# Weight-tile sums by accumulating loads from DRAM, with the seven products in another order

## The chip, the cores and the metric

The kernel runs on one core of a Trainium2 chip. The metric is the device time of one execution, in microseconds (us). Each kernel is run several times and the median is given. One further execution is taken with the hardware profiler; its page and its trace are what the sections below read. The engines are called PE (TensorE, the matrix unit), DVE (VectorE), ACT (ScalarE), POOL (GpSimd) and SP (SyncE) in the profile. SyncE, ScalarE and GpSimd can issue DMA transfers, each on a queue of its own; the transfers of all queues run on the same 16 DMA engines.

## The reference

One layer of a decoder trunk with 256 positions and a width of 2048. All numbers are float32. Cut to what matters here:

```python
h = rmsnorm(x, norm_g)
proj = einsum('bsd,df->bsf', h, w_in)              # 2048 -> 18432, split among four branches
...
ya, yb, yc, yd = ...                               # four token mixers, each times its SiLU gate
yproj = einsum('bsnc,ncd->bsnd', branches, w_branch)
gates = sigmoid(einsum('bsd,df->bsf', h, w_gate) + b_gate)    # 2048 -> 4 * 2048
merged = sum(gates * yproj, axis=2)
out = rmsnorm(x + einsum('bsd,de->bse', merged, w_out), final_g)
```

The change touches the products of `h` with `w_gate` (8192 columns) and with the columns of `w_in` that make the values `a_v` and `c_v` (1024 each).

## The kernel before

**Tiles and precision.** The weights lie in DRAM as tiles of 128 x 2048 float32, 1 MB each. `load_weights` brings one into a buffer of the pool `st`, which has six, on SyncE's queue. TensorE multiplies in float32r, so each operand is cut into a high and a low half by `split` (lines 96 to 98): ScalarE copies the tile to `hi` with rounding, and VectorE takes `lo = st - hi`. There are three buffers for each half. A product is then made of three: high by high, high by low and low by high.

**The products with seven multiplications.** `group` (line 324) computes a block of 256 rows by 1024 columns of `h` times a weight matrix of 2048 rows. It sees both operands as 2 x 2 blocks and uses a scheme of the Strassen-Winograd kind with seven products in place of eight. Four combinations of the blocks of `h` (`s1`, `s2`, `s3`, `n4`) are made once, by `make_sx`. The combinations of the weight blocks are made anew in each group: `tile_of(c, h, j)` loads half `j` of the weight block in row half `h` and column half `c`, and `add_to` (line 340) adds another loaded tile to one that is already in `st`, by one VectorE instruction over 128 x 2048. There are eight such sums in a group, and 12 loads: blocks (1,0) and (1,1), as (c,h), are loaded twice. The sum `ts[j]` is kept for the whole group, and changed in place three times: it starts as block (0,0), and then (1,0), (1,1) and (0,1) are added in turn. A second sum, `t3`, is block (1,0) plus block (1,1).

Every product is two calls of `half` (line 331), each with 12 matmuls of 128 x 512. The products gather in the PSUM banks `X`, `Y` and `Z`; `keep` copies a bank away by ScalarE, and `done` makes the final sums of an output block and hands them to `sink`, which applies the function and writes the result to DRAM (`g_dr` on ScalarE's queue for the gates, `v_dr` on GpSimd's queue for the values).

**The order of work.** `group` is a generator: each `yield` ends a step. Ten groups (eight for the gates, one each for `a_v` and `c_v`) stand in `queue`. The main program goes through the branches; `proj_t` makes the transposed projections, each tile with 32 matmuls, and `branch` multiplies a branch with `w_branch`. Between their tiles they call `step(n)`, which runs the next n steps of the group at the head of the queue. So TensorE's order is written out by hand, in the order in which the program is traced. The order on the other engines comes from a scheduler that follows priorities: `tc.high_priority(SPLIT_AHEAD)` moves splits ahead by 100, `ADD_AHEAD` the sums by 140.

**The other queues.** GpSimd's queue carries the branch values (`y_dr`, `cn`, `yf`, `v`), the gates fetched back (`gl`) and the running sum of the branches (`m_dr`, `ml`). ScalarE's queue carries the gates to DRAM. A queue issues in order: what waits holds up what stands behind it.

Of the kernel before, what the change touches and what calls it, by code (L numbers as in the profile page):

```python
# [9 lines left out]
F32 = mybir.dt.float32  # L10
F32R = mybir.dt.float32r
AF = mybir.ActivationFunctionType
ALU = mybir.AluOpType
AX = mybir.AxisListType

P = 128
# [20 lines left out]
def weight_plan():  # L37

    plan = []
    for n in ("b_a", "b_b", "b_g", "a_q", "a_k", "a_g", "c_u", "c_g", "d_g", "d_q", "d_k"):  # L40
        plan += [("in", OFF[n] // P + i) for i in range(24 if n in ("d_q", "d_k") else 8)]
    for n in ("d_v", "a_v", "c_v"):
        plan += [("inN", OFF[n] // 512 + c, q) for c in range(2) for q in range(4)]
    plan += [("gateN", g, q) for g in range(16) for q in range(4)]
    plan += [("brN", b, c, q) for b in range(4) for c in range(4) for q in range(2)]
    plan += [("out", c, q) for c in range(4) for q in range(4)]
    return plan
# [10 lines left out]
def hybrid_block(ctx: ExitStack, tc, w, x, xT, vec, bg, cst, dmask, sgu_wT, sgu_lg, sgu_lb, sgu_b, final_g, out):  # L58
    nc = tc.nc
    V, A, T = nc.vector, nc.scalar, nc.tensor  # L60
# [16 lines left out]
    ps_n = ctx.enter_context(tc.tile_pool(name="psn", bufs=2, space=bass.MemoryType.PSUM))  # L77
# [4 lines left out]
    index = {e: n for n, e in enumerate(weight_plan())}  # L82
    used = set()

    def load_weights(expect, pieces=1, between=None, again=False):
        assert again == (expect in used), expect
        used.add(expect)
        st = st_p.tile([P, 2048], F32, tag="st", name="st")
        n = 2048 // pieces
        for c in range(pieces):  # L90
            nc.sync.dma_start(st[:, c * n:(c + 1) * n], w[index[expect]][:, c * n:(c + 1) * n])
            if between is not None:
                between(c)
        return st
# [11 lines left out]
    def split_tile(st):  # L106
        hi, lo = new_hi(), new_lo()
        with tc.high_priority(SPLIT_AHEAD):
            split(hi, lo, st[:])
        return hi, lo  # L110
# [207 lines left out]
    def x_part(name):  # L318
        if name in ("a11", "a12", "a22"):
            k0, t0 = (0 if name == "a11" else KB), (P if name == "a22" else 0)  # L320
            return lambda k, part: xhl[:, k0 + k, part * S + t0:part * S + t0 + P]
        return lambda k, part: sx[name][:, part, k, :]

    def group(expect, sink, bias=None):


        def tile_of(c, h, j):
            e = expect(c, 2 * h + j)
            return load_weights(e, again=e in used)

        def half(ps, st, name, j, first, last):
            lh = x_part(name)
            hi, lo = split_tile(st)
            for kk in range(4):
                k, o = 4 * j + kk, kk * 512
                for i, (part, w_) in enumerate(((0, hi), (0, lo), (1, hi))):
                    T.matmul(ps[:], lh(k, part), w_[:, o:o + 512], start=first and j == kk == i == 0,  # L337
                             stop=last and j == 1 and kk == 3 and i == 2, skip_group_check=name not in ("a11", "s1", "a12"))

        def add_to(st, other):  # L340
            with tc.high_priority(ADD_AHEAD):
                V.tensor_add(st[:], st[:], other[:])  # L342

        def keep(ps, name):
            t = so_p.tile([P, 512], F32, tag="so", name=name)
            with tc.high_priority(SPLIT_AHEAD):
                A.activation(t[:], ps[:], AF.Copy)
            return t

        def done(tb, c, op, a, b, t):  # L350
            with tc.high_priority(SPLIT_AHEAD):
                if op is not None:
                    op(t[:], a[:], b[:])
                sink(tb, c, t, op is not None)

        X = ps_x.tile([P, 512], F32, tag="x", name="X")
        if bias is not None:
            T.matmul(X[:], sel[:, bias:bias + 1].to_broadcast([P, P]), bgr[:], start=True, stop=False)
        ts = []
        for j in range(2):  # L360
            ts.append(tile_of(0, 0, j))
            half(X, ts[j], "a11", j, bias is None, True)
            yield
        p1 = keep(X, "p1")
        Z = ps_n.tile([P, 512], F32, tag="n", name="Z")
        if bias is not None:
            T.matmul(Z[:], sel[:, bias + 8:bias + 9].to_broadcast([P, P]), bgr[:], start=True, stop=False)
        for j in range(2):
            add_to(ts[j], tile_of(1, 0, j))
            half(Z, ts[j], "s1", j, bias is None, True)  # L370
            yield
        p5 = keep(Z, "p5")
        for j in range(2):
            add_to(ts[j], tile_of(1, 1, j))
            half(X, ts[j], "s2", j, False, True)
            yield
        u2 = keep(X, "u2")
        for j in range(2):
            t3, b22 = tile_of(1, 0, j), tile_of(1, 1, j)
            half(Z, b22, "n4", j, False, True)  # L380
            add_to(t3, b22)
            yield
            half(X, t3, "s3", j, False, True)
            if j == 0:
                yield
        done(0, 1, V.tensor_sub, Z, u2, u2)
        done(1, 1, V.tensor_sub, p5, X, p5)
        yield
        Y = ps_n.tile([P, 512], F32, tag="n", name="Y")
        for j in range(2):  # L390
            b21 = tile_of(0, 1, j)
            half(Y, b21, "a12", j, True, True)
            add_to(ts[j], b21)
            yield
            half(X, ts[j], "a22", j, False, True)
            if j == 0:
                yield
        done(0, 0, V.tensor_add, Y, p1, p1)
        done(1, 0, None, X, X, X)
        yield  # L400

# [31 lines left out]
    def gate_group(b, cc):  # L433
        bi = BRANCH[b]

        def sink(tb, c, t, in_sbuf):
            g = t if in_sbuf else so_p.tile([P, 512], F32, tag="so", name="g")
            A.activation(g[:], t[:], AF.Sigmoid)
            o = (2 * cc + c) * 512
            nc.scalar.dma_start(g_dr[bi, tb, :, o:o + 512], g[:])  # L440

        return group(lambda c, q: ("gateN", bi * 4 + 2 * cc + c, q), sink, bias=bi * 2 + cc)

    def v_group(name, func):
        def sink(tb, c, t, in_sbuf):
            g = t if in_sbuf else so_p.tile([P, 512], F32, tag="so", name="g")
            if func is not None or not in_sbuf:
                A.activation(g[:], t[:], func or AF.Copy)
            nc.gpsimd.dma_start(v_dr[name][:, tb, c * 512:(c + 1) * 512], g[:])

        return group(lambda c, q: ("inN", OFF[name] // 512 + c, q), sink)
# [395 lines left out]
    for q in range(4):  # L847
        st = load_weights(("out", 3, q))
# [75 lines left out]
```

## Time and profile before

| | us |
|---|---|
| median of 3 runs | 1586.61 |
| lowest and highest run | 1583.34, 1593.16 |
| the profiled execution | 1585.26 |
| its span (first to last instruction) | 1583.4 |

The profiled execution's mean TensorE clock was 0.969 of full speed. In the profile's groups a line reads: line of the kernel, engine, operation, output and inputs, shape, count, then busy time and mean duration, then the idle time of the engine just ahead of them and what ended it. In a list of waits, a row says which instruction waited for which, for how many us in total, how often, and the longest. In a list of DMA issues, the last column is the median time from issue to landing. In the rows of DMA queues stand the packets, the MB moved (10^6 bytes) and the time that the packets took as a share of 16 engines over the span. Matmuls are pipelined: the duration of one is longer than the distance to the next.

### The profile page before, as it was taken

The numbers are of one execution on the slowest core, as the hardware profiler recorded it, in microseconds if no ns is written. First come the engines' busy times: TensorE is split into PE (matmuls) and PEld (weight loads), VectorE is DVE, ScalarE is ACT, GpSimd is POOL, SyncE is SP. The second block draws the span as 40 slices with busy tenths as digits, with TensorE's granted clock in tenths as the row PEclk, the third lists the DMA queues.
The fourth block names the chain that finished last, engine by engine and source line by source line (L and its number), as shares of the span: only waits on it lengthen the run. The fifth ranks groups of instructions, "written<-read, shape, count | busy, mean of one in ns | idle before, by whom it ended". The sixth has DMA issues, their size and how long they took to land.

```text
span 1583.4 us, 18121 instructions
## 1 busy us (share of the span) xinstructions
PE 1465.1 (93%) x7204; PEld 1225.5 (77%) x7204; DVE 1241.8 (78%) x1232; ACT 864.5 (55%) x777; POOL 87.5 (6%) x159
## 2 busy tenths in 40 slices
PE   7999999999999999869999999989989899959897
PEld 6788887888887777658788788867768688847786
DVE  7799999555799998867788788898889777866454
ACT  6544444353457567644466766766554477744251
POOL 0100000000000000010100000000211200011000
PEclk9999999999999999989999999989999999979999
DMA  9655543555166768677876757677898877578441
GB/s 358 217 211 186 186 176 136 180 180 181 59 237 257 283 249 289 212 276 275 283 282 224 241 213 279 239 260 256 301 337 297 328 274 248 196 282 299 167 161 54
DMA packets 62836, 370.89 MB, mean 234 GB/s; under 512 B 8128, under 2 KB 8256, under 8 KB 24096
## 3 DMA queue, kind: packets, MB, share of 16 engines
q1 hardware_dynamic: 44640, 313.68, 54.9%
q0 software_dynamic: 12784, 46.61, 8.8%
q10 hardware_dynamic: 5328, 9.45, 1.7%
q8 instruction: 56, 0.92, 0.2%
q14 instruction: 28, 0.23, 0.0%
HBM read 343.50 MB, written 26.21 MB: 233 GB/s over the span
## 4 chain that ended last, share of the span: by engine, by line
PE 62%; DVE 14%; DMA 10%; issue 7%; ACT 6%; POOL 0%; DVEq 0%; ACTq 0%; POOLq 0%; SPq 0%
PE ps L219 24%; PE ps L222 12%; DVE lo L98 8%; PE X L337 7%; DMA st<-in_w_dram 6%; ACT hi L97 3%; DVE st L342 3%; PE Z L337 3%; PE Y L337 2%; PE pso L261 2%; PE pso L260 2%; PE pso L259 2%; PE psy L259 1%; PE psy L260 1%; PE psy L261 1%
## 5 line engine op out<-in xcount | busy, mean ns | idle before, releaser
L98 DVE TENSOR_TENSOR lo<-st,hi 128x2048 fp32r<-128x2048 f32 (+2 forms) x318 | 711.6, 2247 | 165.7 <-ACT hi L97 164.9
L97 ACT ACTIVATE hi<-st 128x2048 fp32r<-128x2048 f32 (+2 forms) x318 | 595.0, 1879 | 231.4 <-PE psy L261 83.1
L219 PE MATMUL ps<-xhl,hi 128*128 128x512 f32 x1920 | 691.8, 403 | 6.3 <-ACT vd L523 3.8
L222 PE MATMUL ps<-xhl,lo 128*128 128x256 f32 x1920 | 523.4, 283 | 11.3 <-DVE lo L98 11.3
L219 PEld LDWEIGHTS ps<-xhl,hi 128*128 128x128 f32 x1920 | 361.6, 190 | 86.8 <-ACT vd L523 4.2
L222 PEld LDWEIGHTS ps<-xhl,lo 128*128 128x128 f32 x1920 | 366.2, 191 | 24.3 <-DVE lo L98 14.8
L242 ACT ACTIVATE bt<-ps 128x256 f32<-128x256 f32 x120 | 46.0, 384 | 331.0 <-PE ps L219 329.4
L342 DVE TENSOR_TENSOR st<-st 128x2048 f32<-128x2048 f32 x80 | 182.9, 2287 | 33.9 <-DMA st<-in_w_dram 33.5
L337 PE MATMUL X<-hi,xhl 128*128 128x512 f32 x320 | 109.2, 406 | 12.8 <-ACT hi L97 10.9
L337 PE MATMUL X<-hi,s 128*128 128x512 f32 x320 | 106.0, 393 | 0.9 <-ACT hi L97 0.9
L259 PE MATMUL psy<-hi,yh 128*128 128x512 f32 x256 | 100.6, 393 | 5.2 <-DVE ml L792 4.7
L260 PE MATMUL psy<-lo,yh 128*128 128x512 f32 x256 | 100.7, 393 | 1.6 <-DVE lo L98 1.6
L261 PE MATMUL psy<-hi,yl 128*128 128x512 f32 x256 | 100.2, 392 | 0.0
L243 DVE TENSOR_TENSOR dst<-ps,bt 128x256 f32<-128x256 f32 x120 | 50.5, 420 | 61.9 <-ACT bt L242 61.5
L543 DVE SCALAR_TENSOR_TENSOR cv<-glu,vec_sb,cv 128x246 f32<-128x246 f32 (+27 forms) x240 | 98.8, 462 | 0.2
L337 PEld LDWEIGHTS X<-hi,xhl 128*128 128x128 f32 x320 | 63.2, 197 | 27.2 <-ACT hi L97 11.6
L337 PE MATMUL X<-lo,xhl 128*128 128x512 f32 x160 | 65.1, 407 | 7.0 <-DVE lo L98 7.0
L337 PEld LDWEIGHTS X<-hi,s 128*128 128x128 f32 x320 | 60.7, 190 | 13.5 <-ACT hi L97 1.3
L337 PE MATMUL X<-lo,s 128*128 128x512 f32 x160 | 63.5, 397 | 5.6 <-DVE lo L98 5.6
L337 PE MATMUL Y<-hi,xhl 128*128 128x512 f32 x160 | 59.0, 432 | 3.4 <-ACT hi L97 3.4
L337 PE MATMUL Z<-hi,s 128*128 128x512 f32 x160 | 53.7, 400 | 8.7 <-ACT hi L97 8.7
L259 PEld LDWEIGHTS psy<-hi,yh 128*128 128x128 f32 x256 | 48.4, 189 | 16.3 <-DVE ml L792 4.9
(248 smaller groups left out, 1531.6 us busy)
## 6 DMA issues: line engine op xcount, KB each, us to landing
st<-in_w_dram SPq DMA_DIRECT2D x294, 1024.0 KB, 5.4
gl<-g_dr POOLq DMA_DIRECT2D x32, 256.0 KB, 6.8
m_dr<-gl POOLq DMA_DIRECT2D x24, 256.0 KB, 6.1
ml<-m_dr POOLq DMA_DIRECT2D x24, 256.0 KB, 6.3
g_dr<-p ACTq DMA_DIRECT2D x16, 256.0 KB, 4.5
g_dr<-u ACTq DMA_DIRECT2D x8, 256.0 KB, 5.2
g_dr<-g ACTq DMA_DIRECT2D x8, 256.0 KB, 3.9
xr<-in_x_dram POOLq DMA_DIRECT2D x8, 256.0 KB, 4.4
```

The lines of the kernel that those rows point to most:

```text
L97: A.activation(hi, src, AF.Copy)
L98: V.tensor_sub(lo, src, hi.bitcast(F32))
L219: T.matmul(ps[:], hi[:, o:o + P], rhs[:, k, :], start=start, stop=stop)
L222: T.matmul(ps[:, 0:S], lo[:, o:o + P], rhs[:, k, 0:S], start=False, stop=False)
L242: A.activation(bt[:], ps[:, S:2 * S], AF.Copy)
L243: V.tensor_add(dst[:, j, :], ps[:, 0:S], bt[:])
L259: T.matmul(ps[tb][:], lh(k0 + kk, 0, tb), hi[:, o:o + 512], start=st, stop=False)
L260: T.matmul(ps[tb][:], lh(k0 + kk, 0, tb), lo[:, o:o + 512], start=False, stop=False)
L261: T.matmul(ps[tb][:], lh(k0 + kk, 1, tb), hi[:, o:o + 512], start=False, stop=sp)
L337: T.matmul(ps[:], lh(k, part), w_[:, o:o + 512], start=first and j == kk == i == 0, stop=last and j == 1 and kk == 3 and i == 2, skip_grou ...
L342: V.tensor_add(st[:], st[:], other[:])
L543: V.scalar_tensor_tensor(dst, src, wc, dst, op0=ALU.mult, op1=ALU.add)
```

## The change

`add_to` no longer loads a tile and adds it on VectorE. It issues one DMA on GpSimd's queue that reads the tile from DRAM and adds it to what lies in the buffer. The tile that is added is no longer loaded by itself, so a group has 8 plain loads and 8 accumulating ones. Such a transfer may start only when the split of the old content has been read, and the next split waits for it to land.

The products are put in another order. The accumulation for the next use of `ts[j]` is issued right after the step that used it. The product `a12`, which needs no sum, moves from the end to the second place, and its output block is finished there. `n4` and the second sum are cut into two halves, `p3(0)` and `p3(1)`, ahead of and behind `s2`; both tiles of the second sum are kept in `t3s` until `s3`. Block (1,1) is now fetched three times: plainly for `n4`, and by an accumulating load for each of the two sums; before it was fetched twice.

```diff
-        def add_to(st, other):
+        def add_to(st, c, h, j):
+            e = expect(c, 2 * h + j)
+            used.add(e)
             with tc.high_priority(ADD_AHEAD):
-                V.tensor_add(st[:], st[:], other[:])
+                nc.gpsimd.dma_start(st[:], w[index[e]], accum_op=ALU.add)
...
-        ts = []
+        ts, t3s = [], []
         for j in range(2):
             ts.append(tile_of(0, 0, j))
             half(X, ts[j], "a11", j, bias is None, True)
+            add_to(ts[j], 1, 0, j)
             yield
         p1 = keep(X, "p1")
+        Y = ps_n.tile([P, 512], F32, tag="n", name="Y")
+        for j in range(2):
+            half(Y, tile_of(0, 1, j), "a12", j, True, True)
+            if j == 0:
+                yield
+        done(0, 0, V.tensor_add, Y, p1, p1)
+        yield
         Z = ps_n.tile([P, 512], F32, tag="n", name="Z")
...
         for j in range(2):
-            add_to(ts[j], tile_of(1, 0, j))
             half(Z, ts[j], "s1", j, bias is None, True)
+            add_to(ts[j], 1, 1, j)
             yield
         p5 = keep(Z, "p5")
+        def p3(j):
+            half(Z, tile_of(1, 1, j), "n4", j, False, True)
+            t3s.append(tile_of(1, 0, j))
+            add_to(t3s[j], 1, 1, j)
+
+        p3(0)
+        yield
         for j in range(2):
-            add_to(ts[j], tile_of(1, 1, j))
             half(X, ts[j], "s2", j, False, True)
+            add_to(ts[j], 0, 1, j)
             yield
         u2 = keep(X, "u2")
+        p3(1)
+        yield
+        done(0, 1, V.tensor_sub, Z, u2, u2)
         for j in range(2):
-            t3, b22 = tile_of(1, 0, j), tile_of(1, 1, j)
-            half(Z, b22, "n4", j, False, True)
-            add_to(t3, b22)
-            yield
-            half(X, t3, "s3", j, False, True)
+            half(X, t3s[j], "s3", j, False, True)
             if j == 0:
                 yield
-        done(0, 1, V.tensor_sub, Z, u2, u2)
         done(1, 1, V.tensor_sub, p5, X, p5)
         yield
-        Y = ps_n.tile([P, 512], F32, tag="n", name="Y")
         for j in range(2):
-            b21 = tile_of(0, 1, j)
-            half(Y, b21, "a12", j, True, True)
-            add_to(ts[j], b21)
-            yield
             half(X, ts[j], "a22", j, False, True)
             if j == 0:
                 yield
-        done(0, 0, V.tensor_add, Y, p1, p1)
         done(1, 0, None, X, X, X)
         yield
```

## The prediction

> **What bounds the kernel now.** The times of each engine on the page come first, to see which one could be the limit.
>
> ```profile
> PE 1465.1 (93%) x7204; PEld 1225.5 (77%) x7204; DVE 1241.8 (78%) x1232; ACT 864.5 (55%) x777; POOL 87.5 (6%) x159
> ```
>
> TensorE is busy for 93% of the span. Next I asked for the costs by line on VectorE, with a window. The sums that the change removes are the group of line 342; all 80 lie between 468 and 1410 us, so everything below is about these 942 us.
>
> ```profile
> L98 DVE TENSOR_TENSOR lo<-st,hi 128x2048 fp32r<-128x2048 f32 x215 | 489.0, 2287 | 81.8 <-ACT hi L97 81.4
> L342 DVE TENSOR_TENSOR st<-st 128x2048 f32<-128x2048 f32 x80 | 182.9, 2287 | 33.9 <-DMA st<-in_w_dram 33.5
> ```
>
> The third view is the waits of TensorE alone in that window, which tells what VectorE's load costs the engine that is nearly full.
>
> ```profile
> PE Y L337 <- DVE lo L98: 13.7, 5, 3.8
> PE ps L222 <- DVE lo L98: 11.3, 8, 2.8
> PE X L337 <- DVE lo L98: 10.7, 8, 2.2
> PE Z L337 <- ACT hi L97: 8.7, 1, 8.7
> PE Z L337 <- DVE lo L98: 7.2, 7, 1.9
> ```
>
> TensorE waits for a low half from VectorE (line 98) for 13.7 + 11.3 + 10.7 + 7.2 = 42.9 us in all. That is the most that a lighter VectorE can give back directly, although it loses 182.9 us of work. The last view is the busy time in six equal stretches, with the share of the DMA engines, and then the same stretches for line 342 alone.
>
> ```profile
> 468.00:625.00 157.00, 146.13 (x707) 120.48 (x706) 144.36 (x119) 107.91 (x96) 3.85 (x7) 0.99 0.76 272
> 625.00:782.00 157.00, 134.15 (x590) 108.57 (x588) 119.84 (x67) 77.10 (x56) 14.81 (x27) 0.95 0.72 260
> 782.00:939.00 157.00, 153.35 (x776) 130.15 (x777) 128.06 (x82) 103.50 (x90) 2.38 (x4) 0.98 0.72 253
> 939.00:1096.00 157.00, 145.01 (x699) 120.27 (x698) 131.40 (x86) 111.81 (x91) 5.27 (x9) 0.96 0.68 241
> 1096.00:1253.00 157.00, 149.14 (x644) 121.09 (x643) 134.39 (x98) 75.56 (x49) 31.65 (x56) 0.98 0.90 318
> 1253.00:1410.00 157.00, 145.09 (x733) 122.29 (x731) 119.18 (x92) 103.47 (x95) 12.18 (x21) 0.96 0.70 251
> ...
> 468.00:625.00 157.00, 39.91 (x18) 0.99 0.76 272
> 625.00:782.00 157.00, 33.15 (x15) 0.95 0.72 260
> 782.00:939.00 157.00, 29.74 (x13) 0.98 0.72 253
> 939.00:1096.00 157.00, 31.32 (x14) 0.96 0.68 241
> 1096.00:1253.00 157.00, 25.89 (x12) 0.98 0.90 318
> 1253.00:1410.00 157.00, 22.87 (x10) 0.96 0.70 251
> ```
>
> The columns are TensorE, its weight loads, VectorE, ScalarE and GpSimd busy, the clock, the DMA share and GB/s; the last six rows have VectorE's column alone, with the number of sums in brackets (18, 15, 13, 14, 12, 10, together 82: two stand across an edge and count twice). The reader should see that no engine is idle here: the DMA engines already work 0.68 to 0.90 of the time. The change takes work from VectorE and gives it to them.
>
> **The change, part by part.** *The removed sums.* 80 instructions at 2.287 us leave VectorE, 182.9 us. It was not the last to finish except in the 42.9 us above, so this is worth 0 to 42.9 us, and only where nothing else becomes the limit.
>
> In VectorE's program, at the first group of sums (`lo` is a low half, `st` a loaded weight tile, `cv` the convolution), it stands before:
>
> ```order
> L342 TENSOR_TENSOR st<-st 128x2048
> L98 TENSOR_TENSOR lo<-st,hi 128x2048
> L159 TENSOR_SCALAR rs<-rs 128x256
> L243 TENSOR_TENSOR dst<-ps,bt 128x256
> L342 TENSOR_TENSOR st<-st 128x2048
> L98 TENSOR_TENSOR lo<-st,hi 128x2048
> ```
>
> and now:
>
> ```order
> L98 TENSOR_TENSOR lo<-st,hi 128x2048
> L159 TENSOR_SCALAR rs<-rs 128x256
> L160 TENSOR_TENSOR rs<-rs 128x256
> L243 TENSOR_TENSOR dst<-ps,bt 128x256
> L646 TENSOR_TENSOR cv<-cv,rs 128x2048
> L98 TENSOR_TENSOR lo<-st,hi 128x2048 x4
> ```
>
> The splits now follow each other with nothing of the sums between them.
>
> *The loads.* Each of the ten groups loaded 12 tiles of 1 MB on SyncE's queue, and now loads 8, so 40 plain loads go; in their place come 80 accumulating loads on GpSimd's queue. The queue rows price a plain one.
>
> ```profile
> q1 hardware_dynamic: 44640, 313.68, 54.9%
> q0 software_dynamic: 12784, 46.61, 8.8%
> q10 hardware_dynamic: 5328, 9.45, 1.7%
> ```
>
> SyncE's queue (q1) took 0.549 x 1583.4 = 869 us of all 16 engines for 313.68 MB: 2.77 us per MB, or 2.90 us for a tile of 1.049 MB. Where the engines are full, they are a little quicker:
>
> ```profile
> 12.00:42.00 30.00, 26.94 (x117) 21.18 (x116) 25.94 (x28) 19.88 (x25) 0.00 (x0) 1.00 0.99 393
> ...
> 1126.00:1220.00 94.00, 87.73 (x370) 70.97 (x369) 79.00 (x50) 46.99 (x31) 18.75 (x35) 0.96 0.93 329
> ```
>
> At 393 GB/s a tile takes 2.67 us. No accumulating load is in this trace. It must read the tile from DRAM, read the old values from SBUF, and write the sum. From below, the second read costs nothing beside the first: 2.67 us. From above, the two reads and the write each take a pass of their own: 8.0 us. The nearest row for a read of SBUF is ScalarE's queue (q10), whose transfers go from SBUF to DRAM: 0.017 x 1583.4 / 9.45 = 2.85 us per MB, as dear as a read from DRAM. I therefore take two reads in series at the full-engine rate, 2 x 2.67 = 5.3 us, and keep both ends.
>
> [...]
>
> *The sum.* In a stretch with n sums the DMA work becomes share x 157 - (n/2) x 2.90 + n x 5.3 = share x 157 + 3.85 n: 188.6, 170.8, 163.1, 160.7, 187.5 and 148.4 us. Beyond 157 it cannot fit, and the engines do not stay full: the longest full stretch above, 1126 to 1220 us, has 0.93, the short one 0.99. I divide by 0.95: 198.5, 179.8, 171.7, 169.1, 197.4 and 156.2. Over 157 that is 41.5 + 22.8 + 14.7 + 12.1 + 40.4 + 0 = 131.5 us. Where the DMA engines are the limit, the 42.9 us of VectorE are no gain. The span becomes 1583.4 + 131.5 = 1715; the profiled execution took 1585.26 us, 1.9 beyond its span, and lies 1.3 under the median 1586.61. Against the median, 1718 us.
>
> *GpSimd's queue.* Its program at the same place, where `y_dr` and `cn` are branch values stored and fetched, was:
>
> ```order
> L462 DMA y_dr_d<-dst 128x512
> L462 DMA y_dr_b<-cv 128x2048
> L658 DMA cn<-y_dr_b 128x512
> L462 DMA y_dr_b<-dst 128x512
> L658 DMA cn<-y_dr_b 128x512
> ```
>
> and is now:
>
> ```order
> L344 DMA st<-in_w_dram 128x2048
> L471 DMA y_dr_d<-dst 128x512
> L344 DMA st<-in_w_dram 128x2048
> L471 DMA y_dr_b<-cv 128x2048
> L344 DMA st<-in_w_dram 128x2048 x11
> L667 DMA cn<-y_dr_b 128x512
> L344 DMA st<-in_w_dram 128x2048 x3
> ```
>
> The accumulating loads (line 344) stand in one row with the stores and fetches of the branches, and each waits until its tile was split. An issue costs GpSimd what it does now:
>
> ```profile
> L484 POOL DMA_DIRECT2D gl<-g_dr x32 | 17.2, 541 | 60.1 <-DMA m_dr<-gl 35.1 <-PE pt L788 16.1 <-DMA v_dr_c_v<-p 4.2
> ```
>
> 80 x 0.541 = 43 us on an engine that is 6% busy: 0 on the path. SyncE loses 40 issues of an engine that does nothing else, worth 0. What stands behind a waiting accumulation (`gl`, `ml`, `cn`) is late by at most that wait.
>
> *The order of the products.* The matmuls are the same in number, so 0 on TensorE. A tile for the third operand (`t3`) now lives from its step to a later one, two buffers of six in place of a short time. If each of the 20 such tiles held up one load by one half-step of 2.7 us (below), it would cost 55 us; a late load is not among TensorE's five longest waits above, so I take 0 and leave 55 to the range.
>
> **The rivals.** *One read hides the other* (2.67 us): the DMA work is share x 157 + 1.22 n, over 157/0.95 only in the fifth stretch (155.9 / 0.95 = 164.1, +7). Then VectorE's relief is the larger: up to -42.9 + 7 = -36, 1551 us. For it speaks that the tile read from SBUF doesn't use DRAM; against it, that reads of SBUF on q10 are no cheaper per MB.
>
> *Three passes, or short descriptors* (8.0 us): share x 157 + 6.55 n is 237.2, 211.3, 198.2, 198.5, 219.9 and 175.4; over 0.95, beyond 157, together +364: 1950 us. It has for it only that the operation is not in the trace.
>
> *The waits, not the bandwidth.* The chain from a split to the split of the summed tile was 2.29 us of VectorE behind an early load; now it is issue, landing, ScalarE, VectorE. The rows for 1 MB on GpSimd's queue, for ScalarE's half and for one step of TensorE:
>
> ```profile
> yf<-y_dr_a POOLq DMA_DIRECT2D x1, 1024.0 KB, 6.1
> yf<-y_dr_c POOLq DMA_DIRECT2D x1, 1024.0 KB, 9.1
> ...
> L97 ACT ACTIVATE yh<-yf x4: 1909/1910/1921, 700.7 to 1415.1; 128x2048 fp32r<-128x2048 f32 x4
> ...
> 472.32 0.39 PE L337 MATMUL X<-hi,xhl 128*128 128x512 f32 x1
> 477.58 0.39 PE L337 MATMUL X<-hi,xhl 128*128 128x512 f32 x1
> ```
>
> The chain is 0.5 + 6.1 to 9.1 + 1.9 + 2.3 = 10.8 to 13.8 us, and 16 with a second read of 2.67. The last two rows are the first and the last of 24 matmuls: 5.26 / 23 = 0.229 us each, 2.74 for a half-step of 12. Counting TensorE's new order at these rates, 14 to 37 us of other matmuls stand between the use of a tile and of its sum in nearly all of the 60 cases, under 10 us in three. What 16 us lacks there adds up to 43 us: 1630 us, if the DMA engines were not the limit. The order of the products covers most of that wait, so this is unlikely to decide by itself.
>
> **How the numbers follow.** Two reads in series: 0.58, its own range 1650 to 1820 us (4.4 to 6.5 us each in the same sum). One read hidden: 0.18, 1540 to 1600 us. Three passes or worse: 0.16, 1850 to 2100 us. The waits alone: 0.08, 1600 to 1660 us. The likeliest gives 1718 us. From 1575 to 1950 us the range leaves out about 0.11 below and 0.08 above. A measurement of this kernel can tell about 1% from no change, 16 us. Faster by more than that: 0.12, all of the hidden read. Within it: 0.06 of the hidden read and 0.01 of the waits, 0.07. Slower: 0.81.
>
> **What would show it.** The DMA share should be 0.9 or more from 468 us on, to about 1540, and the waits for a low half replaced by waits for `st<-in_w_dram`, by ScalarE above all. Twice the time for the packets of q0 by the MB would confirm 5.3 us; the row of q0 now gives 0.088 x 1583.4 / 46.61 = 3.0 us per MB. VectorE should fall to about 1059 us. I am wrong if the share stays under 0.85 there: then a wait decides, or the sum came cheap.

## The result and the profile after

| | before | after |
|---|---|---|
| median of 4 runs, us | 1586.49 | 1668.95 |
| lowest and highest, us | 1583.34, 1593.16 | 1666.1, 1669.78 |
| span of the profiled execution, us | 1583.4 | 1667.7 |
| mean TensorE clock granted | 0.969 | 0.945 |

The changed kernel is slower: the ratio is 1.0511, with an interval of 1.0475 to 1.0547, or 82 us between the medians. Slower was the forecast; the amount was put at 132 us.

The first part of the page of the changed kernel gives the busy times, and its third part the queues.

```profile
PE 1491.6 (89%) x7204; PEld 1243.3 (75%) x7204; DVE 1073.5 (64%) x1152; ACT 869.1 (52%) x782; POOL 162.7 (10%) x239
...
q1 hardware_dynamic: 38880, 271.74, 43.2%
q0 software_dynamic: 24304, 130.51, 32.6%
```

VectorE lost 168 us of busy time, near the 183 of the sums. GpSimd's queue (q0) went from 8.8% of a shorter span to 32.6%: 543.7 - 139.3 = 404.3 us of all 16 engines for 83.9 MB more, or 4.82 us per MB, 5.05 us for a tile. The difference takes GpSimd's other transfers as unchanged, though they became some 14 us cheaper; the packets of the accumulating loads alone come to 5.22 us a tile. That is near the 5.3 of the forecast. In the trace's records of single packets it can be seen directly: a packet of 8192 bytes on SyncE's queue has a median of 309 ns, one of an accumulating load 628 ns, 2.03 times as much, which fits two reads one after the other.

The stretches of the prediction, now for the changed kernel:

```profile
468.00:625.00 157.00, 131.47 (x610) 107.44 (x609) 94.01 (x90) 90.12 (x82) 15.80 (x20) 0.91 0.96 281
625.00:782.00 157.00, 131.10 (x545) 105.67 (x544) 86.00 (x52) 80.50 (x64) 24.90 (x37) 0.88 0.93 279
782.00:939.00 157.00, 150.40 (x741) 126.15 (x740) 97.99 (x63) 98.18 (x81) 14.31 (x19) 0.99 0.96 304
939.00:1096.00 157.00, 145.54 (x727) 122.86 (x726) 91.73 (x66) 96.66 (x84) 16.65 (x21) 0.97 0.92 261
1096.00:1253.00 157.00, 127.69 (x497) 101.29 (x496) 93.52 (x61) 82.86 (x57) 27.32 (x44) 0.88 0.92 299
1253.00:1410.00 157.00, 139.44 (x680) 116.64 (x679) 96.97 (x86) 88.38 (x75) 30.32 (x39) 0.95 0.91 296
```

The DMA share (the last column but one) was 0.68 to 0.90 and is 0.91 to 0.96 everywhere. TensorE's column fell in five of the six, though the stretches don't hold the same work in both kernels. How far the program has got is read from a transfer that both kernels issue once, the fetch of the last branch's values. Here are its row in the kernel before and in the changed one, each followed by the busy times from 468 us to it:

```profile
L468 POOL DMA_DIRECT2D yf<-y_dr_c x1: 537/537/537, 1406.0 to 1406.0; - x1
468.00:1406.00 938.00, 869.25 (x4124) 720.20 (x4123) 777.23 (x540) 579.35 (x475) 67.52 (x120) 0.97 0.74 266
...
L477 POOL DMA_DIRECT2D yf<-y_dr_c x1: 534/534/534, 1498.4 to 1498.4; - x1
468.00:1498.00 1030.00, 900.86 (x4148) 742.42 (x4146) 611.77 (x460) 589.45 (x485) 141.75 (x198) 0.93 0.93 286
```

The same work took 938 us and takes 1030: 92 us more. TensorE is busy for 32 us of them and idle for 60. The span as a whole grew by 84 us, so all of the loss lies here; behind this transfer the changed kernel is 8 us quicker. The DMA engines' work rose from 0.74 x 938 = 694 to 0.93 x 1030 = 958 us (699 and 964 by the sum of the packets, without rounding).

What this does to the engines shows in ScalarE's waits, since it reads each tile first. The first row is of before, the second of after; then, for the changed kernel, who waited for the accumulating loads (line 344), and who for the plain ones (line 91):

```profile
ACT hi L97 <- DMA st<-in_w_dram: 19.2, 9, 5.7
...
ACT hi L97 <- DMA st<-in_w_dram: 131.5, 28, 12.1
...
  ACT hi L97: 75.9, 16
...
  ACT hi L97: 55.6, 12
```

Of ScalarE's 131.5 us, 75.9 are for 16 of the 80 sums that had not landed, and 55.6 for plain loads that came late. The list of DMA issues has the median times to landing (SyncE's plain loads were at 5.4 us before):

```profile
st<-in_w_dram SPq DMA_DIRECT2D x254, 1024.0 KB, 6.9
st<-in_w_dram POOLq DMA_DIRECT2D x80, 1024.0 KB, 13.1
```

TensorE gets these waits from ScalarE. Here are two of its rows, first of before, then of after:

```profile
PE X L337 <- ACT hi L97: 2.5, 2, 1.6
PE ps L219 <- ACT hi L97: 2.3, 1, 2.3
...
PE X L337 <- ACT hi L97: 25.6, 7, 12.7
PE ps L219 <- ACT hi L97: 16.2, 3, 8.9
```

From 468 us to the fetch, its waits for a high half grew from 16.9 to 49.7 us in all, and those for a low half fell only from 44.5 to 35.3. The profile also follows the chain of work that ended last back from its end. Its shares by engine, before and after:

```profile
PE 62%; DVE 14%; DMA 10%; issue 7%; ACT 6%; POOL 0%; DVEq 0%; ACTq 0%; POOLq 0%; SPq 0%
...
PE 60%; DMA 18%; DVE 7%; ACT 7%; issue 6%; POOL 1%; ACTq 0%; DVEq 0%; POOLq 0%; SPq 0%
```

Sorted by the queue that issued them, SyncE's plain loads hold 90 us of this chain in both kernels, and the accumulating loads 132 us in the changed one; VectorE went from 220 to 121 us. So on this chain the accumulating loads, from issue to landing, have taken the place of work of VectorE, and they take longer.

### The profile page after: what moved, and what is told of

Read it like the earlier page. It is cut to its first block, busy times and chain, and to the rows that moved or that the text cites. A ratio compares the mean times of both kernels' runs of the same rounds, so it can differ in the third digit from the quotient of the medians.

```text
span 1667.7 us, 18214 instructions
## 1 busy us (share of the span) xinstructions
PE 1491.6 (89%) x7204; PEld 1243.3 (75%) x7204; DVE 1073.5 (64%) x1152; ACT 869.1 (52%) x782; POOL 162.7 (10%) x239
## 3 DMA queue, kind: packets, MB, share of 16 engines
q0 software_dynamic: 24304, 130.51, 32.6%
## 4 chain that ended last, share of the span: by engine, by line
PE 60%; DMA 18%; DVE 7%; ACT 7%; issue 6%; POOL 1%; ACTq 0%; DVEq 0%; POOLq 0%; SPq 0%
PE ps L219 23%; DMA st<-in_w_dram 13%; PE ps L222 12%; PE X L337 7%; DVE lo L98 5%; ACT hi L97 4%; PE psy L260 2%; PE psy L261 2%; PE psy L259 2%; PE pso L261 2%; PE Z L337 2%; PE pso L259 2%; PE pso L260 2%; PE Y L337 2%; DMA y_dr_c<-dst 1%
## 5 line engine op out<-in xcount | busy, mean ns | idle before, releaser
L97 ACT ACTIVATE hi<-st 128x2048 fp32r<-128x2048 f32 (+2 forms) x318 | 593.9, 1877 | 310.3 <-DMA st<-in_w_dram 131.5
L337 PE MATMUL X<-hi,s 128*128 128x512 f32 x320 | 115.8, 427 | 23.1 <-ACT hi L97 23.1
L344 POOL DMA_DIRECT2D st<-in_w_dram x80 | 70.4, 906 | 572.3 <-DVE lo L98 409.9
L259 PE MATMUL psy<-hi,yh 128*128 128x512 f32 x256 | 104.8, 410 | 20.1 <-ACT yh L97 10.5
L260 PE MATMUL psy<-lo,yh 128*128 128x512 f32 x256 | 105.1, 410 | 8.2 <-DVE lo L98 8.2
L261 PE MATMUL psy<-hi,yl 128*128 128x512 f32 x256 | 104.5, 408 | 1.2 <-DVE yl L98 1.2
L337 PEld LDWEIGHTS X<-hi,s 128*128 128x128 f32 x320 | 67.2, 210 | 39.1 <-ACT hi L97 25.0
L337 PE MATMUL X<-lo,s 128*128 128x512 f32 x160 | 69.3, 433 | 10.1 <-DVE lo L98 10.1
L337 PE MATMUL Z<-hi,n 128*128 128x512 f32 x160 | 56.1, 413 | 16.2 <-ACT p L349 16.2
L260 PEld LDWEIGHTS psy<-lo,yh 128*128 128x128 f32 x256 | 51.1, 199 | 20.6 <-DVE lo L98 9.6
## 6 DMA issues: line engine op xcount, KB each, us to landing
st<-in_w_dram POOLq DMA_DIRECT2D x80, 1024.0 KB, 13.1
```

What stands on the lines that cost most here:

```text
L97: A.activation(hi, src, AF.Copy)
L259: T.matmul(ps[tb][:], lh(k0 + kk, 0, tb), hi[:, o:o + 512], start=st, stop=False)
L260: T.matmul(ps[tb][:], lh(k0 + kk, 0, tb), lo[:, o:o + 512], start=False, stop=False)
L261: T.matmul(ps[tb][:], lh(k0 + kk, 1, tb), hi[:, o:o + 512], start=False, stop=sp)
L344: nc.gpsimd.dma_start(st[:], w[index[e]], accum_op=ALU.add)
```

## The experiments

Two theories stood against each other. By the first, the accumulating loads fill the DMA engines and the program goes at their pace (throughput). By the second, the chain from split to landing to the next split is too long for the places where the sums stand (waits). Twelve kernels were run. The table has for each the number of accumulating loads, the ratio to the kernel before on the same chip with its interval, the mean DMA share from 468 us to the fetch named above, and how long ScalarE waited for plain loads (line 91) and for tiles of the transfers on GpSimd's queue (line 344).

| kernel | acc. loads | ratio | DMA share | waits for plain, us | waits for sums, us |
|---|---|---|---|---|---|
| before | 0 | 1 | 0.74 | 19.2 | |
| changed | 80 | 1.0511 | 0.93 | 55.6 | 75.9 |
| e1, order only | 0 | 1.0125 [1.0085, 1.0165] | 0.77 | 106.6 | |
| e2, old order | 80 | 1.0740 [1.0703, 1.0776] | 0.92 | 46.9 | 161.4 |
| e4, no second read | 80 plain | 0.9918 [0.9892, 0.9944] | 0.85 | 28.1 | 4.8 |
| h1, t3 on VectorE | 60 | 1.0169 [1.0133, 1.0204] | 0.90 | 51.7 | 19.1 |
| h2, s1 and s2 | 40 | 1.0356 [1.0327, 1.0386] | 0.79 | 17.4 | 117.8 |
| h3, s1 | 20 | 1.0155 [1.0128, 1.0182] | 0.77 | 17.4 | 60.3 |
| e5, a12 second | 0 | 1.0015 [0.9995, 1.0034] | 0.77 | 20.9 | |
| e7, old order, no second read | 80 plain | 1.0001 [0.9978, 1.0024] | 0.85 | 12.6 | 26.5 |
| e9, a22 without second read | 60 + 20 plain | 1.0403 [1.0363, 1.0443] | 0.92 | 49.0 | 66.9 |
| h6, t3 onto n4's tile | 80 | 1.0335 [1.0294, 1.0376] | 0.91 | 35.6 | 97.9 |
| h4, s1 and a22 | 40 | 1.0128 [1.0091, 1.0164] | 0.86 | 50.4 | 1.6 |
| h5, a22 | 20 | 1.0152 [1.0121, 1.0183] | 0.81 | 66.5 | 0 |

**The second read taken away (e4).** Nothing changes but the operation:

```diff
-                nc.gpsimd.dma_start(st[:], w[index[e]], accum_op=ALU.add)
+                nc.gpsimd.dma_start(st[:], w[index[e]])
```

> The changed kernel with accum_op taken away: the same 80 transfers on the same queue with the same waits, but they overwrite (the sums of weight tiles are left out, so the output is another). Throughput theory: 80 x (5.2 - 2.8) = 192 us of DMA work go, about 770 us remain, which fits; with VectorE lighter by 183 us the time falls to 1545 to 1590 us. Rival (the chain of waits): landing falls only from 13 to about 10 us and the chain stays, so it is above 1620 us.

It took 1574.39 us, as the first theory had it, 95 us under the changed kernel. The queue's row and the landing say what went:

```profile
q0 software_dynamic: 24304, 130.51, 23.0%
...
st<-in_w_dram POOLq DMA_DIRECT2D x80, 1024.0 KB, 7.0
```

The queue's time fell from 543.7 us to 0.230 x 1572.3 = 361.6, so what `accum_op` adds, the second read, costs 182.1 / 80 = 2.28 us for a tile. It is seen in its time alone: the queue's megabytes are the same with and without it (130.51), so that the old values are what is read stays an inference. But 182 us of DMA work were worth 95 us of time, about half. And landing fell from 13.1 to 7.0 us, more than the rival had allowed for: with it went the waits for the sums (4.8 us). The run shows that the accumulation in the transfer is the cause of the loss; it doesn't separate the full engines from the late landing.

**The order by itself (e1).** The new order, with each tile loaded plainly and added on VectorE:

```diff
         def add_to(st, c, h, j):
-            e = expect(c, 2 * h + j)
-            used.add(e)
+            other = tile_of(c, h, j)
             with tc.high_priority(ADD_AHEAD):
-                nc.gpsimd.dma_start(st[:], w[index[e]], accum_op=ALU.add)
+                V.tensor_add(st[:], st[:], other[:])
...
-            half(Z, tile_of(1, 1, j), "n4", j, False, True)
+            b22 = tile_of(1, 1, j)
+            half(Z, b22, "n4", j, False, True)
             t3s.append(tile_of(1, 0, j))
-            add_to(t3s[j], 1, 1, j)
+            add_tile(t3s[j], b22)
```

> The new order of the products with the sums on VectorE again (14 plain loads in a group in place of 12, no accumulating load). Throughput theory (the accumulating loads take 2 x the engine time and fill the DMA engines): the DMA work from 468 us on is 697 + 20 x 2.8 = 753 us in about 942, so the time returns to 1585 to 1610 us. Rival (the order and the tiles kept longer cost the time): it stays above 1630 us.

1608.25 us: the throughput theory's number, near its upper end. So the order costs about 1.3% where the sums are on VectorE. ScalarE waits 106.6 us for plain loads, although the DMA engines are busy for only 0.77: the loads land in 5.5 us (5.4 before), so they are issued late, not moved slowly.

**Which part of the order (e5).** The kernel before with only `a12` in the second place, so that its tile has to be loaded again for `a22`:

```diff
         p1 = keep(X, "p1")
+        Y = ps_n.tile([P, 512], F32, tag="n", name="Y")
+        for j in range(2):
+            half(Y, tile_of(0, 1, j), "a12", j, True, True)
...
         for j in range(2):
-            b21 = tile_of(0, 1, j)
-            half(Y, b21, "a12", j, True, True)
-            add_to(ts[j], b21)
-            yield
+            add_to(ts[j], tile_of(0, 1, j))
             half(X, ts[j], "a22", j, False, True)
```

> The kernel before with only a12 moved to the second place, sums on VectorE (14 plain loads in a group; t3 is used in its own step as before). If the 23 us of the order alone come from the two more loads, this has them all: 1600 to 1612 us. If they come from the t3 tiles that live longer, it is near the kernel before: 1583 to 1593 us.

1585.23 us, no difference. The two more loads in a group cost nothing. e1 differs from e5 in two things: `n4` and `t3` are cut in two, with the `t3` tiles kept until `s3`; and each sum, with the load of its second tile, stands right behind the step that used `ts[j]`, not ahead of the one that needs it. Its waits for late loads (106.6 us, here 20.9) fit buffers that come free late. A seventh buffer, which would show it by itself, wasn't tried.

**The old order with accumulating loads (e2), and without their second read (e7).** In e2 the kernel before has its `add_to` replaced by the new one, at the old places; e7 takes `accum_op` away from it.

> The old order with all eight sums of a group as accumulating loads (8 plain and 8 accumulating loads, as in the changed kernel). Throughput theory: the DMA work is the same 960 us, so 1655 to 1690 us. Rival (the wait for an accumulating load to land decides): one or two steps fewer lie between a tile's use and its sum, so it is clearly slower than the changed kernel, 1720 us or more.

> The kernel with the old order and all sums as transfers, with accum_op taken away (the sums of weight tiles are left out). With the run of the new order without the second read it tells what the new order is worth where the DMA engines are not full. If the 37 us between the old and the new order come from the chain of waits alone, they remain: about 1610 us against 1574. If they come only from a chain made longer by full DMA engines, less than 15 us remain: 1575 to 1590 us.

e2 took 1705.51 us, between the two expectations; ScalarE waits 161.4 us for 34 of its sums, twice as long as in the changed kernel. e7 took 1584.98 us against 1574.39 of e4: the old order costs 11 us where the transfers are plain, 37 us where they accumulate. So the new order does what it was arranged for, it covers landing, and most of what it has to cover comes with the second read. e7 says another thing: VectorE is lighter there by 167 us (1074.5 us busy against 1241.8), the engines' share is 0.85, and the time is that of before. Net of the 40 more transfers, the work taken from VectorE was worth nothing in the old order. In the new order it was worth something: e4 takes 34 us less than e1.

**Part of the sums (h1, h2, h3).** h1 is the changed kernel with `t3` on VectorE from the tile of `n4`, as in e1's second part. h2 and h3 are the old order, with the sums for `s1` and `s2`, or `s1` alone, as accumulating loads. In h2 (h3 has the first of these loads only):

```diff
             half(X, ts[j], "a11", j, bias is None, True)
+            acc_to(ts[j], 1, 0, j)
             yield
...
-            add_to(ts[j], tile_of(1, 0, j))
             half(Z, ts[j], "s1", j, bias is None, True)
+            acc_to(ts[j], 1, 1, j)
             yield
...
-            add_to(ts[j], tile_of(1, 1, j))
             half(X, ts[j], "s2", j, False, True)
```

> The changed kernel with the second sum (t3, 20 of the 80) on VectorE again, from the tile that n4 has loaded anyway. Throughput theory: 20 x 5.2 = 104 us of DMA work go, 858 us remain in 942, so most of the loss goes: 1585 to 1620 us. Rival (the chain of waits of the first sum): three quarters of the loss remain, about 1650 us.

> The old order, with only the sums for s1 and s2 (40 of 80) as accumulating loads, each issued right after the step that used the tile; t3 and the sum for a22 stay on VectorE, since their second tile is loaded for a product anyway. Throughput theory: DMA work from 468 us on 697 + 40 x (5.2 - 2.8) = 793 us in about 940, share 0.84, not full; VectorE lighter by 91 us: 1565 to 1600 us. Rival (the chain of waits decides): two steps between use and sum are too few, 1620 us or more.

> The old order, with only the sums for s1 (20 of 80) as accumulating loads. Throughput theory: DMA work 697 + 20 x 2.4 = 745 us, share 0.79; VectorE lighter by 46 us: 1575 to 1595 us, near the kernel before. Rival (the chain of waits decides): 1600 us or more, half of what the kernel with s1 and s2 loses.

h1, at 1614.91 us, came out as the throughput theory had it: 60 accumulating loads cost about 7 us more than e1 without any, and the last 20 cost 54, each net of the sums that VectorE no longer makes. But h2 (1641.19 us) and h3 (1609.46 us) came out as the rival had it. Their engines are far from full on average, 0.79 and 0.77, and yet ScalarE waits 117.8 us for 30 of 40 sums in h2:

```profile
st<-in_w_dram SPq DMA_DIRECT2D x254, 1024.0 KB, 5.8
st<-in_w_dram POOLq DMA_DIRECT2D x40, 1024.0 KB, 10.2
...
  ACT hi L97: 117.8, 30
```

An accumulating load lands after 10.2 us even there, where e7's plain ones on the same queue took 6.6. Two steps of TensorE between use and sum don't cover that. Neither theory is enough alone.

**Less DMA work, with all waits kept (e9), and less work with another chain (h6).** In e9 only the transfers for `a22`, which have the most time, overwrite. In h6 `t3` is made on the tile that `n4` has used, which saves its plain load:

```diff
-            half(Z, tile_of(1, 1, j), "n4", j, False, True)
-            t3s.append(tile_of(1, 0, j))
-            add_to(t3s[j], 1, 1, j)
+            t3s.append(tile_of(1, 1, j))
+            half(Z, t3s[j], "n4", j, False, True)
+            add_to(t3s[j], 1, 0, j)
```

> The changed kernel with accum_op taken away from the transfers for a22 alone (20 of 80; these sums are left out). They have the longest time between issue and use, and every wait stays. Throughput theory (the DMA engines are full at 0.94): work 964 - 20 x 2.4 = 916 us, 916 / 0.94 = 975 in place of 1030, so 1610 to 1630 us. Rival (the waits of the other sums and of the queue decide): hardly any change, 1655 us or more.

> The changed kernel with t3 made by accumulating block (1,0) onto the tile that n4 has just used, so its 20 plain loads go, as does the wait on GpSimd's queue for them. Throughput theory: work 964 - 20 x 2.8 = 908 us, 966 us long: 1600 to 1620 us. Rival (the chains decide): t3 now waits for the split of n4's tile, the time stays above 1645 us.

Both fell between the two expectations: 1649.53 us for e9, 19 us less for 20 x 2.28 = 46 us of work; 1636.99 us for h6, 32 us less for 20 x 2.8 = 56 us of work. In these two a microsecond of DMA work less bought about half a microsecond of time. In e4 it was half as well (95 for 182), but its engines are no longer full, so a part of the 182 us had nothing left to win.

**Sums where there is the most time (h4, h5).** These start from e5, with the sums for `s1` and `a22`, or `a22` alone, as accumulating loads:

```diff
             half(X, ts[j], "s2", j, False, True)
+            acc_to(ts[j], 0, 1, j)
...
-            add_to(ts[j], tile_of(0, 1, j))
             half(X, ts[j], "a22", j, False, True)
```

> The kernel before with a12 in the second place, and the sums for s1 and a22 (40 of 80) as accumulating loads, s2 and t3 on VectorE as before. Between use and sum lie three steps or more, and t3 is not kept. Throughput theory: work 723 + 40 x 2.4 = 819 us, not full; VectorE lighter by 91 us: 1565 to 1592 us. If a landing of 10 us is too late even so: 1600 us or more.

> The same with only the sums for a22 (20 of 80) as accumulating loads, which have the most time between use and sum: work 771 us; VectorE lighter by 46 us; 1570 to 1588 us by the throughput theory, with no wait for a landing. If an accumulating load costs time wherever it stands: 1595 us or more.

1603.88 and 1609.52 us: slower by 1.3 and 1.5%, against what the throughput theory by means says (0.86 and 0.81 are not full), and not by the chain either, since ScalarE waits for no sum at all in h5, and 1.6 us in h4. With 40 accumulating loads h4 is no slower than h5 with 20 (the intervals overlap), so their number alone doesn't decide. In h5 ScalarE waits 66.5 us for plain loads instead, 20.9 in e5, and VectorE 40.6 us for the tiles that it adds, 24.2 in e5. The first such place shows what happens there. Two accumulating loads are issued at 505.27 and 509.74 us; ScalarE's next split waits 8.55 us. The first rows are h5: GpSimd's two issues, ScalarE's wait, and four stretches of 6 us; the last two are e5 in the second and third of these stretches.

```profile
505.27 0.91 POOL L344 DMA_DIRECT2D st<-in_w_dram  x1 [22.09 <-DMA st<-in_w_dram]
509.74 0.88 POOL L344 DMA_DIRECT2D st<-in_w_dram  x1 [3.56 <-DVE lo L98]
...
523.54 1.91 ACT L97 ACTIVATE hi<-st 128x2048 fp32r<-128x2048 f32 x1 [8.55 <-DMA st<-in_w_dram]
...
500.00:506.00 6.00, 6.00 (x33) 4.87 (x32) 6.00 (x9) 5.01 (x4) 0.73 (x1) 1.00 0.98 358
506.00:512.00 6.00, 4.55 (x20) 3.42 (x20) 6.00 (x6) 5.14 (x6) 1.05 (x2) 1.00 1.05 269
512.00:518.00 6.00, 6.00 (x32) 5.08 (x31) 6.00 (x10) 2.99 (x4) 0.00 (x0) 1.00 1.02 233
518.00:524.00 6.00, 5.37 (x28) 4.22 (x26) 0.58 (x2) 0.46 (x1) 0.00 (x0) 1.00 1.00 375
...
506.00:512.00 6.00, 4.56 (x20) 3.44 (x19) 6.00 (x6) 5.09 (x6) 0.00 (x0) 1.00 0.24 102
512.00:518.00 6.00, 6.00 (x33) 5.11 (x32) 6.00 (x9) 3.47 (x5) 0.00 (x0) 1.00 0.88 317
```

From 500 to 524 us h5's engines are full, and they move only 233 to 269 GB/s while the two sums are under way; e5 has 0.24 in the second stretch. The plain loads behind come late, and the next split with them. So at this place the limit is the DMA engines after all, but within 20 us and not as a mean over 157. That the loads can't run far enough ahead to even out a burst, with six buffers of which two hold `ts`, fits this, but it isn't shown: the number of buffers was not changed, and one place was read.

None of the versions that compute the layer beats the kernel before. Only e4 is under it, by 0.8%, and it leaves the sums out.

## Why the prediction was right, and where it was not

*The direction and the mechanism* were right. The accumulating load takes twice the time of a plain one (5.22 us for a tile against 2.68; 5.3 had been taken), the DMA share went to 0.91 to 0.96, and without the second read the loss is gone (e4). Of the signs that were named, the waits for a low half did not go away (44.5 to 35.3 us); ScalarE's for `st` came on top.

*The removed sums* were put at 0 to 42.9 us, and at no gain where the DMA engines are the limit. e7 shows 0 net of its added DMA work, with the engines not full. In e4 TensorE's waits for a low half fell from 44.5 to 22.3 us, so about half of that bound could be won.

*The sum* was too large by 49 us: 131.5 forecast, 82 measured. For the stretch that it was made for, from 468 us on, 92 us is the number to compare; the 8 us gained behind it were not in the sum. Two of its terms were mis-sized. The DMA work was forecast as 1019 us and came out as 964 by the packets. The largest part is the plain loads, which became cheaper: 2.68 us for a tile in place of 2.88, 32 us for the 160 or so in the window. The other transfers fell from 115 to 102 us, the stretches counted 82 sums in place of 80 (8 us), and the accumulating loads cost 5.22 and not 5.3 us (6 us). I held the price of the plain loads constant while adding slower traffic beside them. The other term is the pace: 0.95 was taken and 0.93 measured. The two errors have opposite signs, so a part of the sum came near by luck. The form of the sum was also too simple. It holds the program to the engines' pace by means over 157 us. Less work of 46 and 56 us bought about half of itself (e9, h6), and 20 sums cost 1.5% at a mean share of 0.81 (h5).

*The order of the products* was put at 0, with 55 us left to the range for the `t3` tiles. e1 shows 23 us for the order with VectorE's sums, and e5 none for `a12`'s part. It does not follow that the order is a part of the 82 us: where the sums are transfers, the new order saves time, 37 us from e2 to the changed kernel and 11 us from e7 to e4.

*The waits* were called unlikely to decide by themselves, and the sum has no term for them. That parted the two theories too cleanly. The chain was priced with a landing of 6.1 to 9.1 us and 2.67 more; it was 13.1 with the engines full, and 10.2 or more with them not full, so that 16 sums came late and cost ScalarE 75.9 us, and the accumulating loads hold 132 us of the chain of work that ended last. In the old order the waits decide with the engines not full (h2, h3).

*One read hidden* is out by the packets, 628 ns against 309; *three passes* are out by the same. GpSimd's issue went from 0.54 to 0.91 us on average for an accumulating load, and stayed off the path as forecast:

```profile
L344 POOL DMA_DIRECT2D st<-in_w_dram x80 | 70.4, 906 | 572.3 <-DVE lo L98 409.9 <-DMA st<-in_w_dram 118.2 <-issue 32.1
```

The same row has what the forecast lacked: GpSimd's queue stood for 118.2 us behind loads, 113.4 of them behind the plain ones of `t3`, with other sums behind. Removing that (h6) came with 32 us, together with 56 us of DMA work; the two were not separated.

*What stays open*: how the 82 us divide between full engines and late sums, since the time to landing is longer where the DMA share is higher (10.2 us for an accumulating load in h2, at 0.79, and 13.1 in the changed kernel, at 0.93; the chain, one path among many, points at the sums: its share of plain loads did not grow); and how much of e1's 23 us comes from buffers, how much from the two `n4` steps, and how much from the earlier places of the sums.

## What to carry to other kernels

Here an accumulating load moved a sum of 2.29 us from VectorE to the DMA engines, at twice the DMA time of a plain load (5.22 us for a tile against 2.68). No run shows it pay. By what they do show, it would need a place where VectorE ends last and where the DMA engines have room for that time, in the very stretch where the sums stand. A mean over a stage does not show this room: h5 lost 1.5% at a mean share of 0.81, with a full stretch of 24 us inside. And before moving work off an engine, look at what waits for it: by TensorE's waits 42.9 us was the most to win from 183 us of VectorE, and e4 freed 22 of them.

## What the runs showed of the hardware

Around two of TensorE's waits, 2.36 and 1.82 us long, near 605 us in the changed kernel, the granted clock fell: 0.89 over the 6 us that hold the first, 0.55 over the next 6. The rows are TensorE's two waits and two stretches with all engines:

```profile
604.20 0.50 PE L337 MATMUL X<-hi,s 128*128 128x512 f32 x1 [2.36 <-ACT hi L97]
606.53 0.79 PE L337 MATMUL X<-lo,s 128*128 128x512 f32 x1 [1.82 <-DVE lo L98]
...
600.00:606.00 6.00, 2.35 (x10) 1.36 (x8) 1.82 (x1) 3.76 (x3) 1.04 (x2) 0.89 1.06 298
606.00:612.00 6.00, 5.47 (x14) 4.32 (x15) 5.81 (x5) 2.83 (x4) 1.43 (x2) 0.55 1.03 213
```

TensorE did only 10 matmuls in the first 6 us, and its 14 in the next 6 us kept it busy for 5.47. Over the whole span the same 7204 matmuls were busy for 1491.6 us in place of 1465.1, so 26 of the 84 us of span are longer matmuls and 58 are idle time. Ahead of the fall came waits of 1.72 us (it ended at 599.06 us) and 2.36 us, 3 us apart. The mean clock is lower in the kernels in which ScalarE waits longest for tiles, 0.969 before (19.2 us), 0.945 after (131.5) and 0.937 in e2 (208.2), but not in strict order: e1 has 0.966 with 106.6 us of these waits, h1 0.961 with 70.8.
